# Seven block products in part of down, q, k and v, with q and k computed token-major

## The chip, the cores and the metric

The kernel runs on one core of one Trainium2 chip. The metric is device time in microseconds, the median of several runs; three runs of the kernel before gave 1916.19 us (1915.48 to 1917.2).

## The reference

The reference is a decoder trunk of two layers on 256 tokens of width 2048, in float32. Layer 0 mixes tokens with a causal pooling mixer, layer 1 with differential attention; each is followed by a SwiGLU FFN of width 5632, and the result is normalised.

```python
h = h + pool_mixer(rmsnorm(h), pool_w, pool_scale)              # layer 0
h = h + (silu(n @ wg) * (n @ wu)) @ wd                          # n = rmsnorm(h)
h = h + diff_attention(rmsnorm(h), w_qkv, ..., w_o)             # layer 1
h = h + (silu(n @ wg) * (n @ wu)) @ wd
out = rmsnorm(h, final_norm)
# diff_attention, for each of 8 heads: q and k have two parts of 128, v has 256 columns
p_c = softmax(q_c k_c^T * 128 ** -0.5 - slope * distance, causal)    # c = 0, 1
o = rmsnorm((p_0 - lam * p_1) v, subln_g) * (1 - lambda_init)
```

## The kernel before, in words

**The split.** Every weight and every operand is held as two parts that TensorE multiplies at full rate, a rounded high part and the rest as a low part. A product of two blocks is three matmuls: high x high, high x low, low x high. A weight tile `raw` of 128 x 2048 (1 MB) comes by DMA; `halves` (L105 to L110) rounds it on ACT (`whi`, L108) and subtracts on DVE (`wlo`, L109). Both have three buffers, and so has `raw`.

**Groups.** A group (L128 to L164) makes a result of 256 tokens x 1024 columns: four blocks C11, C12, C21, C22 of 128 tokens x 512 columns in four PSUM banks. It runs over steps of 256 rows of the weight, eight of them for most matrices. A plain step has eight block products, 24 matmuls of 512 columns. A step in seven products has seven block products (the scheme of Strassen in Winograd's form), 21 matmuls; it needs sums of weight blocks (`tsum`, L114 to L117, split into `thi` on ACT and `tlo` on DVE, L120 and L121) and sums of operand blocks. Its products go to seven banks M1, M6, M7, P5, P3, P4, M2, of which the last three are shared with the plain steps as C12, C21 and C11; the eighth bank, X, takes C22 of the plain steps. A group with such steps uses all eight PSUM banks, and `combined` (L166 to L193) makes the four blocks from them, with two copies on ACT and eight adds on DVE. `SEVEN` names the steps: 0, 1 and 4, in gate/up only.

**PSUM.** There are eight banks. `acc` turns through banks 0 to 4, `aux` through 5 to 7. In a group C11, C12, C21 and C22 stand in banks 6, 4, 5 and 7, and M1, M6, M7, P5 in 0 to 3. Transposes, scores and small products take banks from `aux`.

**Stages.** The pooling mixer (L252 to L329) fills `x_tok`, the residual, and transposes it into the operand of FFN 0. An FFN (L331 to L392) has 11 gate/up groups of eight steps, in chunks of 4, 4 and 3. After each the gate goes through Silu on ACT, is multiplied by up on DVE (L351), transposed by TensorE (L357) and split (L359, L360). After a chunk two down groups of 8, 8 or 6 steps are added to `x_tok` (L374). The last chunk also squares `x_tok` and transposes it into the next operand. In attention, q and k were computed unit by unit with the weight as the stationary operand (`product`, L419 and L421): 32 units of 1 MB, each 16 matmuls of 512 columns and 16 of 256, so that q and k come out already transposed, in banks 0 to 4. The two halves of a unit's result are added (L471 to L477) and k is scaled by a row. After a head's four units come its scores (L487), softmax (L489 to L503) and the transposes of its probabilities (L437). Then two groups of v, in plain steps, each followed by four heads (L519 to L535), and two groups of the output product.

**Order.** The program is written stage after stage, and a scheduler puts each engine's instructions into one fixed queue, by readiness in its own model and by priority; a buffer that is still in use holds back the instruction that wants it. The engines run these queues strictly in order, with semaphores between them. So an instruction that waits holds back all that stands behind it on its engine.

Of the kernel before, what the change touches and what calls it, by code (L numbers as in the profile page):

```python
# [16 lines left out]
P = 128  # L17
# [6 lines left out]
H = 8  # L24
# [10 lines left out]
SEVEN = (0, 1, 4)  # L35
# [9 lines left out]
def trunk_kernel(ctx, tc, x_t, x_n, gains, scale_in, final_in, subln, lam_in, band, dist,  # L45
# [41 lines left out]

    def operand(seven=()):

        return [resid.tile([P, 2, 8, P] if p in seven else [P, 2, 2, S], F32R, name="xp", tag=f"xp{p}")  # L90
                for p in range(NP)]
# [20 lines left out]
    def sums(pool, raw):  # L112
        t = pool.tile([P, 4, 512], F32, name="tsum")
        nc.vector.tensor_tensor(t[:, T1:T3 + 1], raw[:, B11:B22 + 1],  # L114
                                raw[:, B12:B12 + 1].broadcast_to([P, 2, 512]), ALU.add)
        nc.vector.tensor_tensor(t[:, T2], t[:, T1], raw[:, B22], ALU.add)
        nc.vector.tensor_tensor(t[:, T4], t[:, T2], raw[:, B21], ALU.add)  # L117
        hi = pool.tile([P, 4, 512], F32R, name="thi")
        lo = pool.tile([P, 4, 512], F32R, name="tlo")
        nc.scalar.copy(hi, t)  # L120
        nc.vector.tensor_tensor(lo, t, f32(hi), ALU.subtract)  # L121
        return hi, lo
# [5 lines left out]
    def group(steps, seven_pool=None):  # L128
# [37 lines left out]
    def combined(ps, pool=None):  # L166
# [3 lines left out]
        get = lambda name, tag, bufs: pool.tile([P, 512], F32, name=name, tag=tag, bufs=bufs)  # L170
        m1 = get("m1", "m", 2)
        nc.scalar.copy(m1, ps[M1])
        u2 = get("u2", "u", 2)
        nc.vector.tensor_tensor(u2, ps[M6], m1, ALU.add)
        c11 = get("c11", "c", 4)
        nc.vector.tensor_tensor(c11, ps[M2], m1, ALU.add)
        u3 = get("u3", "u", 2)
        nc.vector.tensor_tensor(u3, ps[M7], u2, ALU.add)
        p5 = get("p5", "m", 2)
        nc.scalar.copy(p5, ps[P5])  # L180
        q = get("q", "q", 2)
        nc.vector.tensor_tensor(q, p5, u2, ALU.subtract)
        c12 = get("c12", "c", 4)
        nc.vector.tensor_tensor(c12, ps[P3], q, ALU.add)
        c21 = get("c21", "c", 4)
        nc.vector.tensor_tensor(c21, ps[P4], u3, ALU.add)
        q2 = get("q2", "q", 2)
        nc.vector.tensor_tensor(q2, p5, u3, ALU.subtract)
        if X not in ps:
            return [[c11, c12], [c21, q2]]  # L190
        c22 = get("c22", "c", 4)
        nc.vector.tensor_tensor(c22, ps[X], q2, ALU.add)
        return [[c11, c12], [c21, c22]]  # L193
# [31 lines left out]

    def transposed(xp, j, gain, seven=()):

        for p in (2 * j, 2 * j + 1):
            ps = aux((P, 2, 2, P))
            for i in range(2):  # L230
                cols = slice((2 * p + i) * P, (2 * p + i + 1) * P)
                for t in range(2):
                    at = 1 - t if p in seven else t
                    nc.tensor.transpose(ps[:, i, at], x_tok[:, t, cols], ident)
            g = [gain_sb[:, gain, 2 * p + i:2 * p + i + 1] for i in range(2)]
            if p not in seven:
                for i in range(2):
                    split(xp[p][:, i], ps[:, i].rearrange("p t s -> p (t s)"), g[i])
                continue
            e = tmp.tile([P, 8, P], F32, name="e", bufs=1)  # L240

            nc.scalar.activation(e[:, A21:A11 + 1], ps[:, 0], AF.Copy, scale=g[0])
            nc.scalar.activation(e[:, A22], ps[:, 1, 0], AF.Copy, scale=g[1])
            nc.scalar.activation(e[:, A12], ps[:, 1, 1], AF.Copy, scale=g[1])
            nc.vector.tensor_tensor(e[:, S1:S3 + 1], e[:, A21:A11 + 1], e[:, A22:A21 + 1], ALU.subtract)
            nc.vector.tensor_tensor(e[:, S2], e[:, S1], e[:, A11], ALU.subtract)
            nc.vector.tensor_tensor(e[:, S4], e[:, A12], e[:, S2], ALU.add)
            nc.scalar.copy(xp[p][:, 0], e)
            nc.vector.tensor_tensor(xp[p][:, 1], e, f32(xp[p][:, 0]), ALU.subtract)
# [81 lines left out]
    def ffn(layer, xq, ss, seven, next_op, next_gain):  # L331
# [3 lines left out]
        with tc.tile_pool(name=f"ffn{layer}", bufs=1, reuse_waits="tile") as hp:  # L335
            g0 = 0
            for c, n in enumerate(CHUNKS):
                last = c == len(CHUNKS) - 1
                hp_tiles = []
                if last and next_op is None:  # L340
                    final_sb = [hp.tile([P, 1024], F32, name="final_sb", tag=f"h3_{i}") for i in range(2)]
                    for i in range(2):
                        nc.scalar.dma_start(out=final_sb[i], in_=final_in[:, i * 1024:(i + 1) * 1024])
                for g in range(g0, g0 + n):
                    ps = group([(xq[p], p in seven, w_gu[layer][g, p]) for p in range(NP)], hp)
                    cs = combined(ps, hp)
                    h = hp.tile([P, 2, 512], F32, name="h")
                    for t in range(2):
                        a = cs[t][0] if seven else hp.tile([P, 512], F32, name="silu", bufs=2)
                        nc.scalar.activation(a, cs[t][0], AF.Silu, scale=r[:, t:t + 1])  # L350
                        nc.vector.scalar_tensor_tensor(h[:, t], cs[t][1], r[:, t:t + 1], a, ALU.mult, ALU.mult)  # L351
                    for i in range(2):
                        ht = hp.tile([P, 2, 2, S], F32R, name=f"h{g - g0}_{i}")
                        tp = aux((P, 2, S))
                        for k in range(2):
                            for t in range(2):
                                nc.tensor.transpose(tp[:, k, t * P:(t + 1) * P],  # L357
                                                    h[:, t, (2 * i + k) * P:(2 * i + k + 1) * P], ident)
                        nc.scalar.copy(ht[:, :, 0], tp)  # L359
                        nc.vector.tensor_tensor(ht[:, :, 1], tp, f32(ht[:, :, 0]), ALU.subtract)  # L360
                        hp_tiles.append(ht)
                for o in range(2):
# [5 lines left out]
                    ps = group([(hp_tiles[i], False, w_down[layer][o, 2 * g0 + i]) for i in range(2 * n)])  # L368
                    cs = combined(ps, hp)
                    for b in range(2):  # L370
# [6 lines left out]
                        if last and next_op is not None:  # L377
                            transposed(next_op, j, next_gain)
                g0 += n
            if next_op is None:  # L380

                r = row_scale(ss_next)
                for j in range(4):
                    cols = slice(j * 512, (j + 1) * 512)
                    y = hp.tile([P, 2, 512], F32, name="y", tag=f"h{j // 2}_{j % 2}")
# [8 lines left out]
    xp = operand()  # L394
    ss = ffn(0, xq, ss, SEVEN, xp, 3)
# [3 lines left out]
    with tc.tile_pool(name="attn", bufs=1, reuse_waits="tile") as ap_, ExitStack() as heads:  # L399
        at = heads.enter_context(tc.tile_pool(name="attn_tmp", bufs=2, reuse_waits="tile"))  # L400
        v_sb = ap_.tile([P, 2, D], F32, name="v_sb")
        r_col = row_scale(ss)
        qk = ap_.tile([P, 4, S], F32, name="qk0", tag="qk", bufs=8)
        qs_col = ap_.tile([P, 2], F32, name="qs_col")
        subln_sb = ap_.tile([P, 2], F32, name="subln_sb")
        nc.sync.dma_start(out=subln_sb, in_=subln)
        lam_sb = ap_.tile([P, 4], F32, name="lam_sb")
        nc.sync.dma_start(out=lam_sb, in_=lam_in)
        nc.vector.tensor_scalar(qs_col, r_col, QK_SCALE, None, ALU.mult)
        r = None  # L410
        neg_lam = None
        aT = []

        def product(src, acts):

            ps = acc((P, 2, S))
            hi, lo = (x.rearrange("p b (u n) -> p (b u) n", n=P) for x in halves(load(src)))
            for k, a in enumerate(acts):
# [221 lines left out]
```

## Time and profile before

| what | value |
|---|---|
| median of three runs | 1916.19 us |
| the profiled execution | 1915.97 us |
| its span | 1914.2 us |
| granted TensorE clock, mean | 0.993 |
| TensorE busy | 1871.7 us, 98% |
| VectorE busy | 1344.9 us, 70% |
| ScalarE busy | 921.3 us, 48% |

PE is TensorE, PEld its weight loads, DVE VectorE, ACT ScalarE, SP the queue that issues the DMAs. The span goes from the first to the last instruction of one profiled execution. A row of the groups by line has the line, the engine, the operation, what is written <- what is read, the shapes and the count, then busy us and mean ns of one, and the idle time ahead with what ended it. A row of the stages has the window, its length, and for PE, PEld, DVE, ACT and POOL busy us and count, then the granted clock (1 is full), the share of the DMA engines and GB/s. A row of the timeline has start, length, engine and line; in brackets stands the idle time before it and who ended it. Matmuls overlap in the records (each lasts some 390 ns there and the next starts after some 228), so the spacing of starts is what a matmul costs.

### The profile page before, as it was taken

The numbers are of one execution on the slowest core, as the hardware profiler recorded it, in microseconds if no ns is written. First come the engines' busy times: TensorE is split into PE (matmuls) and PEld (weight loads), VectorE is DVE, ScalarE is ACT, GpSimd is POOL, SyncE is SP. The second block draws the span as 40 slices with busy tenths as digits, with TensorE's granted clock in tenths as the row PEclk, the third lists the DMA queues.
The fourth block names the chain that finished last, engine by engine and source line by source line (L and its number), as shares of the span: only waits on it lengthen the run. The fifth ranks groups of instructions, "written<-read, shape, count | busy, mean of one in ns | idle before, by whom it ended". The sixth has DMA issues, their size and how long they took to land.

```text
span 1914.2 us, 20836 instructions
## 1 busy us (share of the span) xinstructions
PE 1871.7 (98%) x8508; PEld 1526.5 (80%) x8508; DVE 1344.9 (70%) x1311; ACT 921.3 (48%) x892; POOL 0.7 (0%) x6
## 2 busy tenths in 40 slices
PE   8899999999999999999999999999999999999997
PEld 5678888888888888888887787788888888888886
DVE  5898756888558975666654356898558897468854
ACT  5555534455434545544445545555434554345543
POOL 0000000000000000000000000000000000000000
PEclk9999999999999999999999999999999999999999
DMA  7455555555556564555553454555555556565552
GB/s 284 154 198 198 197 180 198 195 198 198 195 188 211 176 207 169 177 174 177 174 186 137 139 176 157 189 203 199 198 195 201 198 176 211 185 219 198 198 194 92
DMA packets 51151, 358.83 MB, mean 187 GB/s; under 512 B 6000, under 2 KB 6256, under 8 KB 8432
## 3 DMA queue, kind: packets, MB, share of 16 engines
q1 hardware_dynamic: 50080, 355.36, 53.3%
q10 hardware_dynamic: 976, 2.15, 0.3%
q8 instruction: 66, 1.08, 0.2%
q14 instruction: 29, 0.24, 0.0%
HBM read 355.39 MB, written 2.10 MB: 187 GB/s over the span
## 4 chain that ended last, share of the span: by engine, by line
PE 93%; DVE 3%; ACT 2%; DMA 1%; issue 1%; SPq 0%; DVEq 0%; ACTq 0%
PE b L162 80%; PE b L419 6%; PE b L421 3%; PE b L357 1%; DVE wlo L109 1%; ACT whi L108 1%; DMA x_tok<-x_n 1%; PE b L297 1%; PE b L487 1%; ACT sq L212 0%; PE b L533 0%; PE b L307 0%; DVE xp L224 0%; DMA raw<-w_gu 0%; ACT o_sq L525 0%
## 5 line engine op out<-in xcount | busy, mean ns | idle before, releaser
L109 DVE TENSOR_TENSOR wlo<-raw,whi 128x2048 fp32r<-128x2048 f32 (+1 forms) x331 | 721.3, 2182 | 354.8 <-ACT whi L108 354.0
L108 ACT CAST whi<-raw 128x2048 fp32r<-128x2048 f32 (+1 forms) x331 | 603.1, 1825 | 607.6 <-PE b L162 511.1
L162 PE MATMUL b<-whi,xp 128*128 128x512 f32 x2412 | 768.4, 392 | 6.5 <-DVE xp L224 3.9
L162 PEld LDWEIGHTS b<-whi,xp 128*128 128x128 f32 x2412 | 453.2, 188 | 104.4 <-issue 5.1
L162 PE MATMUL b<-wlo,xp 128*128 128x512 f32 x1206 | 470.7, 390 | 1.8 <-DVE wlo L109 1.8
L162 PE MATMUL b<-whi,h 128*128 128x512 f32 x1408 | 438.3, 391 | 0.0
L162 PEld LDWEIGHTS b<-whi,h 128*128 128x128 f32 x1408 | 263.7, 188 | 56.8 <-DVE h L360 2.1
L162 PE MATMUL b<-wlo,h 128*128 128x512 f32 x704 | 274.2, 390 | 0.1
L162 PEld LDWEIGHTS b<-wlo,xp 128*128 128x128 f32 x1206 | 226.9, 188 | 50.0 <-DVE wlo L109 3.0
L121 DVE TENSOR_TENSOR tlo<-tsum,thi 128x2048 fp32r<-128x2048 f32 x66 | 151.1, 2290 | 52.6 <-ACT thi L120 51.7
L162 PE MATMUL b<-thi,xp 128*128 128x512 f32 x528 | 185.1, 397 | 2.4 <-ACT thi L120 2.3
L419 PE MATMUL b<-xp,whi 128*128 128x512 f32 x512 | 183.1, 402 | 0.0
L120 ACT CAST thi<-tsum 128x2048 fp32r<-128x2048 f32 x66 | 126.1, 1910 | 99.5 <-DVE tsum L117 77.0
L162 PEld LDWEIGHTS b<-wlo,h 128*128 128x128 f32 x704 | 132.2, 188 | 27.3 <-DVE wlo L109 0.5
L421 PE MATMUL b<-xp,wlo 128*128 128x256 f32 x512 | 138.0, 280 | 0.0
L162 PEld LDWEIGHTS b<-thi,xp 128*128 128x128 f32 x528 | 97.2, 189 | 28.7 <-ACT thi L120 10.9
L419 PEld LDWEIGHTS b<-xp,whi 128*128 128x128 f32 x512 | 95.0, 188 | 19.8
L162 PE MATMUL b<-tlo,xp 128*128 128x512 f32 x264 | 105.4, 399 | 0.0
L421 PEld LDWEIGHTS b<-xp,wlo 128*128 128x128 f32 x512 | 96.6, 189 | 2.6
L162 PE MATMUL b<-whi,oT 128*128 128x512 f32 x256 | 81.5, 397 | 0.5 <-DVE xp L224 0.5
L114 DVE TENSOR_TENSOR tsum<-raw 128x1024 f32<-128x1024 f32 x66 | 80.5, 1220 | 0.6
L162 PEld LDWEIGHTS b<-tlo,xp 128*128 128x128 f32 x264 | 50.0, 189 | 13.7 <-DVE tlo L121 3.2
(122 smaller groups left out, 1016.7 us busy)
## 6 DMA issues: line engine op xcount, KB each, us to landing
raw<-w_gu SPq DMA_DIRECT2D x176, 1024.0 KB, 4.8
raw<-w_down SPq DMA_DIRECT2D x88, 1024.0 KB, 4.8
raw<-w_qk SPq DMA_DIRECT2D x32, 1024.0 KB, 4.8
raw<-w_v SPq DMA_DIRECT2D x16, 1024.0 KB, 4.8
raw<-w_o SPq DMA_DIRECT2D x16, 1024.0 KB, 4.8
raw<-pool_w SPq DMA_DIRECT2D x3, 1024.0 KB, 16.9
x_tok<-x_n SPq DMA_DIRECT2D x1, 2048.0 KB, 14.2
xf<-x_t SPq DMA_DIRECT2D x3, 512.0 KB, 10.8
```

Of the source, the lines that this page charges most:

```text
L108: nc.scalar.copy(hi[:, lo_block:], raw[:, lo_block:])
L109: nc.vector.tensor_tensor(lo[:, lo_block:], raw[:, lo_block:], f32(hi[:, lo_block:]), ALU.subtract)
L114: nc.vector.tensor_tensor(t[:, T1:T3 + 1], raw[:, B11:B22 + 1], raw[:, B12:B12 + 1].broadcast_to([P, 2, 512]), ALU.add)
L120: nc.scalar.copy(hi, t)
L121: nc.vector.tensor_tensor(lo, t, f32(hi), ALU.subtract)
L162: nc.tensor.matmul(ps[b], x, y[:, block], start=first, stop=(left[b] == 0))
L297: nc.tensor.matmul(zp[g][t], u, w[:, k % 4], start=(k % 4 == 0 and i == 0), stop=(k % 4 == 3 and i == 2))
L357: nc.tensor.transpose(tp[:, k, t * P:(t + 1) * P], h[:, t, (2 * i + k) * P:(2 * i + k + 1) * P], ident)
L419: big = lambda: nc.tensor.matmul(ps.rearrange("p a s -> p (a s)"), hi[:, k], a.rearrange("p a s -> p (a s)"), start=(k == 0), stop=(k == N ...
L421: small = lambda: nc.tensor.matmul(ps[:, 0, :], lo[:, k], a[:, 0, :], start=False, stop=False)
L487: nc.tensor.matmul(sc[:, :nk], qk[:, c, qb * P:(qb + 1) * P], qk[:, 2 + c, :nk], start=True, stop=True)
```

## The change

**Where the seven products are.** In gate/up the seven steps are now 1, 4 and 6. In each down group they are steps 1 and 4, in each group of q and k and of v steps 1 and 4; the output product stays plain. The transposes that make the operands go through one helper, `pair`, for `x_tok`, the product of gate and up and the attention output alike; for a seven step it forms the sums of operand blocks (`e`) on ACT and DVE.

**q and k.** The units are gone. There are four groups of q and k like the others, with 512 columns of q as the left blocks and 512 of k as the right ones, so one group holds two heads. Its blocks are combined (in place, in four tiles of one buffer each), scaled by row on ACT, transposed by TensorE (L470) and copied by ACT (L472); then each head runs as before, with the scale already in q. The heads are written behind their group, ahead of the next.

**Smaller edits.** `combined` works in place. The sums of a seven step are made ahead of the split of the same tile. The scalars of attention share one tile. The gate and up product is written over up. The probabilities have three blocks in place of four, v stays in the combined tiles.

```diff
-SEVEN = (0, 1, 4)
+SEVEN = (1, 4, 6)
+SEVEN_DOWN = (1, 4)
+SEVEN_QKV = (1, 4)
+SEVEN_O = ()
...
             raw = load(src)
+            t = sums(pool, raw) if seven else None
             w = [halves(raw, B11 if seven else 0)]
             if seven:
-                w.append(sums(seven_pool, raw))
+                w.append(sum_halves(pool, t))
...
+        m1, u2, u3, p5 = (pool.tile([P, 512], F32, name=f"c{i}") for i in ("11", "12", "21", "22"))
         nc.scalar.copy(m1, ps[M1])
         nc.vector.tensor_tensor(u2, ps[M6], m1, ALU.add)
+        nc.vector.tensor_tensor(m1, ps[M2], m1, ALU.add)
         nc.vector.tensor_tensor(u3, ps[M7], u2, ALU.add)
         nc.scalar.copy(p5, ps[P5])
+        nc.vector.tensor_tensor(u2, p5, u2, ALU.subtract)
+        nc.vector.tensor_tensor(p5, p5, u3, ALU.subtract)
+        nc.vector.tensor_tensor(u2, ps[P3], u2, ALU.add)
+        nc.vector.tensor_tensor(u3, ps[P4], u3, ALU.add)
+        if X in ps:
+            nc.vector.tensor_tensor(p5, ps[X], p5, ALU.add)
+        return [[m1, u2], [u3, p5]]
...
+    def pair(dst, src, gains, seven):
+        ps = aux((P, 2, 2, P))
+        for i in range(2):
+            for t in range(2):
+                nc.tensor.transpose(ps[:, i, 1 - t if seven else t], src(i, t), ident)
...
+        e = tmp.tile([P, 8, P], F32, name="e", bufs=1)
+        for i, at in ((0, slice(A21, A11 + 1)), (1, slice(A22, A12 + 1, A12 - A22))):
+            nc.scalar.activation(e[:, at], ps[:, i], AF.Copy, scale=1.0 if gains is None else gains[i])
+        nc.vector.tensor_tensor(e[:, S1:S3 + 1], e[:, A21:A11 + 1], e[:, A22:A21 + 1], ALU.subtract)
+        nc.vector.tensor_tensor(e[:, S2], e[:, S1], e[:, A11], ALU.subtract)
+        nc.vector.tensor_tensor(e[:, S4], e[:, A12], e[:, S2], ALU.add)
+        nc.scalar.copy(dst[:, 0], e)
+        nc.vector.tensor_tensor(dst[:, 1], e, f32(dst[:, 0]), ALU.subtract)
...
-                    ps = group([(hp_tiles[i], False, w_down[layer][o, 2 * g0 + i]) for i in range(2 * n)])
-                    cs = combined(ps, hp)
+                    cs = combined(group([(hp_tiles[i], i in SEVEN_DOWN, w_down[layer][o, 2 * g0 + i])
+                                         for i in range(2 * n)], hp), hp)
...
-                big = lambda: nc.tensor.matmul(ps.rearrange("p a s -> p (a s)"), hi[:, k], a.rearrange("p a s -> p (a s)"),
-                                               start=(k == 0), stop=(k == NK - 1))
-                small = lambda: nc.tensor.matmul(ps[:, 0, :], lo[:, k], a[:, 0, :], start=False, stop=False)
...
-            for i in range(4):
-                ps = product(w_qk[h * 4 + i], acts)
-                if i == 1 and probs is not None:
-                    transpose_probs(h - 1, probs)
...
+        for g in range(4):
+            cs = combined(group([(xp[p], p in SEVEN_QKV, w_qk[g, p]) for p in range(NP)], ap_), ap_)
+            for t in range(2):
+                for b, scale in enumerate((qs_col, r_col)):
+                    nc.scalar.activation(cs[t][b], cs[t][b], AF.Copy, scale=scale[:, t:t + 1])
+            for u in range(2):
+                qk = at.tile([P, 2, 2, S], F32, name="qk", bufs=3)
+                for b in range(2):
+                    tp = aux((P, 2, S))
+                    for c in range(2):
+                        for t in range(2):
+                            nc.tensor.transpose(tp[:, c, t * P:(t + 1) * P],
+                                                cs[t][b][:, (2 * u + c) * P:(2 * u + c + 1) * P], ident)
+                    nc.scalar.copy(qk[:, b], tp)
+                head(2 * g + u, qk)
...
-            cs = combined(group([(xp[p], False, w_v[g, p]) for p in range(NP)]))
+            cs = combined(group([(xp[p], p in SEVEN_QKV, w_v[g, p]) for p in range(NP)], ap_), ap_)
```

More of the change, by code (lines that the diff above doesn't have):

```diff
@@ L224, in split @@
         nc.vector.scalar_tensor_tensor(dst[:, 1, :], src, gain, f32(dst[:, 0, :]), ALU.mult, ALU.subtract)
+    def pair(dst, src, gains, seven):
[3 more added lines that the diff above has]
+                nc.tensor.transpose(ps[:, i, 1 - t if seven else t], src(i, t), ident)
+        if not seven:
+            if gains is None:
+                both = ps.rearrange("p i t s -> p i (t s)")
+                nc.scalar.copy(dst[:, :, 0], both)
+                nc.vector.tensor_tensor(dst[:, :, 1], both, f32(dst[:, :, 0]), ALU.subtract)
+            else:
+                for i in range(2):
+                    split(dst[:, i], ps[:, i].rearrange("p t s -> p (t s)"), gains[i])
+            return
+        e = tmp.tile([P, 8, P], F32, name="e", bufs=1)
[6 more added lines that the diff above has]
+        nc.vector.tensor_tensor(dst[:, 1], e, f32(dst[:, 0]), ALU.subtract)
@@ L226, in transposed @@
     def transposed(xp, j, gain, seven=()):
         for p in (2 * j, 2 * j + 1):
[L229 to L239, printed above, removed]
@@ L248, in transposed @@
-            nc.scalar.copy(xp[p][:, 0], e)
-            nc.vector.tensor_tensor(xp[p][:, 1], e, f32(xp[p][:, 0]), ALU.subtract)
+            pair(xp[p], lambda i, t: x_tok[:, t, (2 * p + i) * P:(2 * p + i + 1) * P],
+                 [gain_sb[:, gain, 2 * p + i:2 * p + i + 1] for i in range(2)], p in seven)
     xp = operand()
```

181 lines of the change are left out of this document (52 added, 129 removed).

## The prediction

> **What bounds the kernel now.** I read the page first, then the table of stages (the windows), then the chain of waits, then the groups by line and shape, and last the timeline of the places that the change touches.
>
> The page gives the span, PE's busy time and the chain that ended last.
>
> ```profile
> span 1914.2 us, 20836 instructions
> PE 1871.7 (98%) x8508; PEld 1526.5 (80%) x8508; DVE 1344.9 (70%) x1311; ACT 921.3 (48%) x892; POOL 0.7 (0%) x6
> PE 93%; DVE 3%; ACT 2%; DMA 1%; issue 1%; SPq 0%; DVEq 0%; ACTq 0%
> ```
>
> PE is the bound: 93% of the chain is matmul time. A matmul that goes away takes its whole slot with it, unless PE then waits for something else. In the stages (start:end, length, PE, weight load, DVE, ACT, POOL, granted clock, DMA) PE is full in a gate/up group and in the stretch of q and k, and only the seams have holes.
>
> ```profile
> 628.00:671.00 43.00, 43.00 (x197) 35.25 (x196) 38.30 (x34) 22.98 (x18) 0.00 (x0) 1.00 0.57 196
> 782.00:975.00 193.00, 193.00 (x1116) 168.54 (x1115) 126.75 (x232) 91.24 (x151) 0.00 (x0) 1.00 0.50 173
> 1180.00:1206.00 26.00, 22.24 (x99) 16.36 (x98) 21.18 (x30) 17.56 (x24) 0.00 (x0) 0.99 0.47 161
> ```
>
> DVE, the second engine, stands at 38.3 of 43 us in a gate/up group, so seven-product steps already run it near full. The slot of a matmul comes from the chain of waits (start, length): 548 matmuls in 124.70 us are **0.2276 us** each. Below it are the scores of two heads that lie seven heads apart: (974.12 - 805.50) / 7 = **24.09 us a head**.
>
> ```profile
> 242.36 124.70 PE b L162 x548
> 805.50 0.66 PE b L487 x4
> 974.12 0.66 PE b L487 x4
> ```
>
> **The change part by part.** The profiled execution took 1915.97 us with a span of 1914.2, and the median of the runs is 1916.19, 0.2 above it; the sum is made against 1915.97.
>
> *Down and v.* A seven-product step has 21 matmuls for 24. Down has 12 groups with two such steps each, 72 matmuls less, -16.4 us; v has two groups, 12 less, -2.7 us. What they add lies on DVE and ACT: sums of weights, their split, and the recombination.
>
> ```profile
> L109 DVE TENSOR_TENSOR wlo<-raw,whi 128x2048 fp32r<-128x2048 f32 x265 | 606.5, 2289 | 349.1 <-ACT whi L108 349.0
> L109 DVE TENSOR_TENSOR wlo<-raw,whi 128x1536 fp32r<-128x1536 f32 x66 | 115.7, 1753 | 5.7 <-ACT whi L108 5.0
> L121 DVE TENSOR_TENSOR tlo<-tsum,thi 128x2048 fp32r<-128x2048 f32 x66 | 151.1, 2290 | 52.6 <-ACT thi L120 51.7
> L114 DVE TENSOR_TENSOR tsum<-raw 128x1024 f32<-128x1024 f32 x66 | 80.5, 1220 | 0.6
> L117 DVE TENSOR_TENSOR tsum<-tsum,raw 128x512 f32<-128x512 f32 x66 | 45.5, 690 | 1.6
> ```
>
> A plain step costs DVE 2.29 us against 5.46 of PE (24 slots); a seven step costs 1.75 + 2.29 + 1.22 + 2 x 0.69 = 6.64 against 4.78. A down group of eight steps is then 2 x 6.64 + 6 x 2.29 + 8 recombining adds and 4 adds to x_tok at 0.69 = 35.3 us of DVE for 42.3 of PE. It fits, and since the M banks are complete after step 4, five adds run under the last steps. The six-step group of the last chunk is 30.7 for 31.4: it fits without slack.
>
> *q and k, the work of PE.* Before, two heads take 48.2 us. After, a group of two heads has 186 matmuls (42.3 us), 16 transposes of q and k, 6 of the probabilities, and 8 scores. Timeline rows: six transposes from 241.49 to 242.11 are 0.10 each; four scores are 0.47 + 0.55 (each pair starts here and the next L419 at 805.80 and 807.65).
>
> ```profile
> 241.49 0.87 PE L357 MATMUL b<-ident,h 128*128 128x128 f32 x6
> 242.11 0.48 PE L162 MATMUL b<-whi,h 128*128 128x512 f32 x1
> 805.33 0.82 PE L487 MATMUL b<-qk 128*128 128x128 f32 x4
> 805.80 0.58 PE L419 MATMUL b<-xp,whi 128*128 128x512 f32 x1
> 807.10 0.89 PE L487 MATMUL b<-qk 128*128 128x128 f32 x4
> 807.65 0.58 PE L419 MATMUL b<-xp,whi 128*128 128x512 f32 x1
> ```
>
> 42.3 + 2.2 + 2.0 = 46.6 us for 48.2, so -1.6 x 4 = -6.1 us (unrounded) if nothing waits. The DVE of a group: before, 126.75 / 193 x 48.2 = 31.7. Three kinds of x16 like the row below go (12 of 0.42 a group), two seven steps (+8.7) and eight adds (+5.5) come: 40.8 of 46.6.
>
> ```profile
> L476 DVE TENSOR_TENSOR k_s<-b,q_c 128x256 f32<-128x256 f32 x16 | 6.7, 420 | 14.5 <-ACT q_c L471 14.5
> ```
>
> The loads cost nothing either way: 32 of 1 MB before and after, in the same queue.
>
> ```profile
> raw<-w_qk SPq DMA_DIRECT2D x32, 1024.0 KB, 4.8
> ```
>
> *q and k, the waits.* Here the order changes most. Before, products of q and k used banks 0 to 4, and heads 5 to 7. On PE, two scores stand among unit products that need nothing of the head:
>
> ```order
> L419 MATMUL b2_5444<-xp_449,whi_5447 128x512
> L421 MATMUL b2_5444<-xp_449,wlo_5448 128x256 x2
> L419 MATMUL b2_5444<-xp_449,whi_5447 128x512
> L487 MATMUL b7_5490<-qk0_5294 128x128 [waits DVE_49,PE_49]
> L487 MATMUL b6_5517<-qk0_5294 128x256 [waits Activation_49]
> L419 MATMUL b3_5545<-xp_442,whi_5548 128x512 [waits Activation_49]
> ```
>
> After, on PE at the second head of the first group (a_sb are the probabilities, qk the transposed q and k, xp_439 the next group's first step):
>
> ```order
> L470 MATMUL b5_5794<-ident_75,c22_5696 128x128
> L423 MATMUL b6_5781<-ident_75,a_sb_5751 128x128 [waits DVE_49]
> L438 MATMUL b7_5813<-qk_5787 128x128 [waits Activation_49]
> L438 MATMUL b5_5829<-qk_5787 128x256 [waits PE_49]
> L423 MATMUL b6_5781<-ident_75,a_sb_5778 128x128 [waits DVE_49]
> L423 MATMUL b6_5781<-ident_75,a_sb_5778 128x128
> L438 MATMUL b6_5802<-qk_5787 128x128 [waits PE_49,Activation_49]
> L438 MATMUL b6_5840<-qk_5787 128x256 [waits DVE_49]
> L172 MATMUL b5_5883<-whi_5865,xp_439 128x512 [waits DVE_49]
> L172 MATMUL b5_5883<-wlo_5866,xp_439 128x512
> L172 MATMUL b5_5883<-whi_5865,xp_439 128x512
> L172 MATMUL b6_5869<-whi_5865,xp_439 128x512 [waits DVE_49]
> ```
>
> A group now takes all eight banks, so the next group's banks 5, 6, 7 are closed until the heads give them back. Nothing stands between these head rows, and five of the eight wait for DVE or ACT. Their cost from rows (DVE neighbours overlap by some 0.08 us: 857.04 + 0.48 is past 857.43):
>
> ```profile
> 857.04 0.48 DVE L489 SCALAR_TENSOR_TENSOR s_sb<-b,qs_col,bias 128x256 f32<-128x256 f32 x1
> 857.43 0.15 DVE L496 RECIPROCAL l_inv<-l_sum 128x1 f32<-128x1 f32 x1
> L491 DVE TENSOR_REDUCE m_neg<-s_sb 128x1 f32<-128x256 f32 x16 | 6.5, 404 | 0.0
> L494 ACT ACTIVATE p_sb<-s_sb,m_neg 128x256 f32<-128x256 f32 x16 | 8.0, 503 | 20.1 <-DVE m_neg L491 20.1
> L503 DVE SCALAR_TENSOR_TENSOR a_sb<-p_sb,l_inv 128x256 f32<-128x256 f32 x8 | 3.9, 485 | 0.3
> L438 ACT COPY aT<-b 128x256 f32<-128x256 f32 x8 | 3.0, 375 | 1.9 <-PE b L437 1.9
> ```
>
> I walked the three queues by hand from the group's last matmul (0). The sums c11, c12, c21 are done before 0, because DVE waits there only for ACT's casts; c22 at 2.4; then one wlo (2.2) and the first tsum (1.2) keep DVE until 5.8, when it takes the first scores. PE has 27 matmuls, 16 transposes and four scores until 9.2, with holes of 0.3 in all. Then it waits 0.4 for a_sb (9.5), 0.9 for ACT's copy of q and k, which queues behind two exps (10.5), 0.4 for the next a_sb (11.4), 0.8 until ACT has taken bank 6, 0.5 and 0.8 for the scores to be read (13.1, 14.2). At 17.7 both heads are done, with 13.6 us of PE work in it: **4.1 us idle a group, +16.5 us** for four (the last before v's first group). DVE then owes the next weight split, done at 22.7; PE has matmuls until 24.1. Bounds: 2 us, if handovers are quicker than I took them, and 9, if each costs more and the holes add up. The nearest row is the heads after v's first half, where a chain over the same engines leaves PE 4.2 of 16 us idle, so I keep 4.1.
>
> ```profile
> 1021.00:1037.00 16.00, 11.79 (x54) 8.58 (x53) 7.71 (x27) 12.07 (x37) 0.00 (x0) 1.00 0.30 110
> ```
>
> Such holes can cost clock too. After v's second half PE waits 1.43 and 0.93 us in short succession, and then the granted clock is 0.57 for four us:
>
> ```profile
> 1090.37 0.91 PE L533 MATMUL b<-ident,o_n 128*128 128x128 f32 x4 [1.43 <-ACT o_n L529]
> 1092.21 1.04 PE L533 MATMUL b<-ident,o_n 128*128 128x128 f32 x4 [0.93 <-ACT o_n L529]
> 1092.50:1096.50 4.00, 3.96 (x13) 3.20 (x13) 1.45 (x3) 1.34 (x4) 0.00 (x0) 0.57 0.00 0
> ```
>
> 0.43 x 4 us is 1.7 us lost each time. In v's first half (row above) the clock stayed at 1.00, so I take 0.6 x 4 x 1.7 = **+4**. The Trainium skill ("TensorE: Matmul & The Clock Gate", Part 1 and the table "Why this matters for your kernels") states that the clock drops after an idle window of about 3.4 us and warns of gaps over some 3 us; by that rule the heads, with no hole over 1 us, lose nothing. The row above disagrees: holes of 1.43 and 0.93 were enough. What the rule would make of the time is a rival below.
>
> *Gate/up.* The steps in seven products are 1, 4, 6 for 0, 1, 4: equal work, other order. Before, at the seam, a new group opened bank 0, which is free early (names as above):
>
> ```order
> L162 MATMUL b7_873<-whi_1007,xp_98 128x512
> L162 MATMUL b0_1090<-whi_1078,xp_91 128x512 [waits Activation_49]
> L162 MATMUL b0_1090<-wlo_1079,xp_91 128x512 [waits DVE_49]
> L162 MATMUL b0_1090<-whi_1078,xp_91 128x512
> L162 MATMUL b6_1094<-whi_1078,xp_91 128x512 [waits DVE_49]
> ```
>
> After, PE opens banks 6 and 4 at once and then wants c12, the product of gate and up:
>
> ```order
> L172 MATMUL b7_795<-whi_1003,xp_98 128x512
> L172 MATMUL b6_1071<-whi_1067,xp_91 128x512 [waits DVE_49,Activation_49]
> L172 MATMUL b6_1071<-wlo_1068,xp_91 128x512
> L172 MATMUL b6_1071<-whi_1067,xp_91 128x512 x2
> L172 MATMUL b4_1078<-whi_1067,xp_91 128x512 [waits DVE_49]
> L231 MATMUL b7_1050<-ident_75,c12_1032 128x128 [waits DVE_49]
> ```
>
> The reader sees 11 matmuls (2.5 us) ahead of the transpose. By the same walk DVE ends the last tlo at -10.3, bank 6's add at -3.3, bank 4's at 0.9, c12 at 2.1: **0**, with 0.4 us to spare. If DVE is 0.8 us later, 22 groups cost +9.
>
> *Seams.* At o to FFN 1 and at the start of FFN 0 the first step is now plain, and its PE work covers the sums of step 1.
>
> ```profile
> 1187.69 0.47 PE L162 MATMUL b<-whi,xp 128*128 128x512 f32 x1 [1.01 <-DVE xp L224]
> 1194.02 1.20 PE L162 MATMUL b<-thi,xp 128*128 128x512 f32 x4 [0.93 <-ACT thi L120]
> 1203.62 1.20 PE L162 MATMUL b<-thi,xp 128*128 128x512 f32 x4 [1.12 <-ACT thi L120]
> 1205.43 1.60 PE L162 MATMUL b<-whi,xp 128*128 128x512 f32 x3 [0.61 <-ACT whi L108]
> 1206.00:1208.00 2.00, 2.00 (x6) 1.62 (x5) 2.00 (x1) 0.00 (x0) 0.00 (x0) 0.50 0.03 8
> 62.00:64.00 2.00, 0.65 (x5) 0.41 (x4) 2.00 (x5) 1.70 (x6) 0.00 (x0) 1.00 0.00 0
> 66.00:68.00 2.00, 2.00 (x6) 1.52 (x6) 1.74 (x7) 0.91 (x2) 0.00 (x0) 0.50 0.00 0
> ```
>
> These holes are 3.7 us and a clock loss of 1.7; about 1.5 stays (bank 5 waits for the splits of x_tok), -3.9. The start has some 2.9 and 1.7 of the same kind; I take -3.1. Together **-7** (bounds -10 and 0). At FFN 0 to q/k the other way: x_tok and two e chains come later by the adds, step 1's tsum waits behind them, **+3.5** with the last chunk (0 to +8). At the end one add more stands before the last x_tok add: **+0.6**.
>
> Sum: -16.4 - 2.7 - 6.1 + 16.5 + 4 + 0 - 7 + 3.5 + 0.6 = -7.6, so 1908.4, with the 0.2 to the median 1908.6.
>
> **The rivals.**
> *Heads exposed (slower).* The walk's waits each come longer, since a group's heads sit on one chain over three engines and PE's queue is in order. For it: five waits in eight rows. Against it: of other work only two short sums of weights stand inside the heads on DVE, none on ACT. It decides from 4.1 + (7.6 + 3.8) / 4 = 7 us idle a group; at 9 us and with a clock loss each time it is 1908.6 + 19.6 + 2.8 = 1931. Chance 0.22.
> *DVE becomes the bound in down.* The last chunk's groups have 30.7 for 31.4 us, and in FFN 0 the splits of x_tok come on top: three plain pairs of two like the row below, and a seven pair of about 2.2 us (estimated from the rows of its shapes above), 5.1 of DVE for 1.6 of PE, 2.8 too much in each of two groups. That gives 1914. Against: the adds under the last step already use DVE's idle time. Chance 0.16.
>
> ```profile
> L224 DVE SCALAR_TENSOR_TENSOR xp<-b,gain_sb,xp 128x256 fp32r<-128x256 f32 x36 | 15.8, 477 | 1.6 <-ACT xp L223 1.6
> ```
>
> *The waits are hidden.* PE's matmuls cover the heads but for 1 us a group, clock kept: 1908.6 - 12.4 - 4 = 1892. Chance 0.10.
> *No clock loss.* The heads keep the full clock as in v's first half: 1904.6. Chance 0.12; this is where the skill's rule would put it.
>
> **How the numbers follow.** The forecast itself has 0.40; its own range is 1902 to 1915. About 0.2% (3.8 us) is what a measurement of this kernel can tell from no change. Faster than 1912.4: most of the forecast (0.34), both hidden cases (0.22) and a little of DVE's (0.04): 0.60. Within: the rest of the forecast and DVE's case, 0.18. Slower: 0.22. The range, 1891 to 1930, holds the hidden heads at its lower end and the exposed ones nearly at its upper.
>
> **What would show it.** Right: PE matmuls of down, v and q/k fewer by 84 and replaced as counted; two heads in some 51 us, with PE idle of 3 to 6 us after each group of q and k, released by DVE a_sb and s_sb and ACT's copies; gate/up groups still at some 43 us; the holes at 62 to 68 and 1187 to 1208 smaller. Wrong: gate/up groups over 43.3 us, down groups of eight steps over 43, idle per group of heads under 2 or over 7, or a granted clock of one half in other places.

## The result and the profile after

The kernel after took 1900.91 us (median of four runs, 1899.33 to 1903.71) against 1916.63 for the kernel before: ratio 0.9921, 95% interval 0.9909 to 0.9933, or -15.1 us (0.8%) where -7.6 was forecast. The profiled execution took 1902.04. The page now reads:

```profile
span 1900.1 us, 20741 instructions
PE 1852.9 (98%) x8204; PEld 1506.3 (79%) x8204; DVE 1571.1 (83%) x1591; ACT 1013.6 (53%) x983; POOL 0.7 (0%) x6
PE 92%; DVE 4%; ACT 2%; issue 1%; DMA 1%; SPq 0%; DVEq 0%; ACTq 0%
```

PE is still the bound. DVE has 226 us more to do. In the chain of waits (start, length) the transposes behind two gate/up groups of FFN 0, and the long stretch of matmuls in the second, third and fourth group of q and k and in the first group of v:

```profile
366.36 0.66 PE b L231 x6
409.09 0.66 PE b L231 x6
...
834.69 33.15 PE b L172 x145
885.55 33.17 PE b L172 x145
936.42 33.11 PE b L172 x145
988.27 33.11 PE b L172 x145
```

A gate/up group takes 42.7 us. From one of these stretches to the next, a group with its two heads, it is 50.9, 50.9 and 51.9 us, where the forecast had some 51. The timeline of PE at the second head of the second group:

```profile
877.72 0.92 PE L438 MATMUL b<-qk 128*128 128x128 f32 x4 [0.43 <-ACT qk L472]
878.78 0.44 PE L423 MATMUL b<-ident,a_sb 128*128 128x128 f32 x2
879.85 0.49 PE L438 MATMUL b<-qk 128*128 128x128 f32 x2 [0.63 <-ACT aT L425]
880.73 0.70 PE L438 MATMUL b<-qk 128*128 128x256 f32 x2 [0.38 <-DVE s_sb L440]
881.64 0.50 PE L172 MATMUL b<-whi,xp 128*128 128x512 f32 x1 [0.21 <-DVE s_sb L440]
```

PE stands in this order, in front of ACT's copies and the scores being read, as walked. The brackets sum to 1.65 us, yet 878.78 to 879.85 is 1.07 us for two transposes: a record ends later than the slot it needs, so part of a wait lies under it. The granted clock (next to last but two) behind three such stretches:

```profile
828.00:832.00 4.00, 3.59 (x9) 2.60 (x10) 3.21 (x15) 1.81 (x8) 0.00 (x0) 0.59 0.00 0
880.00:884.00 4.00, 3.40 (x15) 2.38 (x16) 3.39 (x17) 1.97 (x8) 0.00 (x0) 1.00 0.02 4
982.00:986.00 4.00, 3.62 (x10) 2.60 (x10) 3.43 (x16) 1.97 (x8) 0.00 (x0) 0.57 0.00 0
```

It drops in the first and last group, not in the two between (from 930 to 934 us it is 1.00 too). At the seam from o to FFN 1, PE's waits from 1180 to 1290 in the kernel before (total, times, longest):

```profile
PE b L162 <- ACT thi L120: 2.0, 2, 1.1
PE b L162 <- DVE xp L224: 1.0, 1, 1.0
PE b L162 <- DVE wlo L109: 0.9, 1, 0.9
PE b L162 <- ACT whi L108: 0.6, 1, 0.6
```

and all that is left at the same place in the kernel after:

```profile
PE b L172 <- DVE xp L224: 0.5, 1, 0.5
```

### The profile page after: what moved, and what is told of

It is laid out like the page before. It is cut to its first block, busy times and chain, and to the rows that moved or that the text cites. A ratio compares the mean times of both kernels' runs of the same rounds, so it can differ in the third digit from the quotient of the medians.

```text
span 1900.1 us, 20741 instructions
## 1 busy us (share of the span) xinstructions
PE 1852.9 (98%) x8204; PEld 1506.3 (79%) x8204; DVE 1571.1 (83%) x1591; ACT 1013.6 (53%) x983; POOL 0.7 (0%) x6
## 4 chain that ended last, share of the span: by engine, by line
PE 92%; DVE 4%; ACT 2%; issue 1%; DMA 1%; SPq 0%; DVEq 0%; ACTq 0%
PE b L172 88%; PE b L231 2%; DVE wlo L115 1%; DMA x_tok<-x_n 1%; PE b L303 1%; ACT sq L212 1%; ACT whi L114 1%; PE b L313 0%; PE b L438 0%; DVE tsum L120 0%; DVE y L386 0%; DVE x_tok L373 0%; DVE s_sb L440 0%; DVE oT L224 0%; DVE xp L224 0%
## 5 line engine op out<-in xcount | busy, mean ns | idle before, releaser
L172 PE MATMUL b<-whi,xp 128*128 128x512 f32 x2804 | 905.8, 393 | 8.8 <-DVE c L189 3.0
L172 PEld LDWEIGHTS b<-whi,xp 128*128 128x128 f32 x2804 | 526.9, 189 | 126.9 <-ACT e L244 5.7
L172 PE MATMUL b<-wlo,xp 128*128 128x512 f32 x1402 | 549.9, 392 | 0.6 <-DVE wlo L115 0.5
L172 PE MATMUL b<-whi,h 128*128 128x512 f32 x1168 | 370.3, 390 | 1.1 <-ACT e L244 1.1
L130 DVE TENSOR_TENSOR tlo<-tsum,thi 128x2048 fp32r<-128x2048 f32 x102 | 233.1, 2286 | 19.8 <-ACT thi L129 19.3
L172 PE MATMUL b<-wlo,h 128*128 128x512 f32 x584 | 227.5, 390 | 0.1
L129 ACT CAST thi<-tsum 128x2048 fp32r<-128x2048 f32 x102 | 194.8, 1910 | 30.7 <-DVE tsum L123 30.7
L122 DVE TENSOR_TENSOR tsum<-tsum,raw 128x512 f32<-128x512 f32 x102 | 70.4, 690 | 2.4
L123 DVE TENSOR_TENSOR tsum<-tsum,raw 128x512 f32<-128x512 f32 x102 | 70.1, 687 | 1.9
L172 PEld LDWEIGHTS b<-tlo,xp 128*128 128x128 f32 x312 | 58.6, 188 | 12.1 <-DVE tlo L130 0.2
L172 PE MATMUL b<-thi,h 128*128 128x512 f32 x192 | 67.6, 393 | 0.3 <-ACT thi L129 0.3
L172 PEld LDWEIGHTS b<-whi,oT 128*128 128x128 f32 x256 | 49.2, 193 | 12.9 <-issue 2.6
```

Source lines behind the costliest of these rows:

```text
L172: nc.tensor.matmul(ps[b], x, y[:, block], start=first, stop=(left[b] == 0))
```

## The experiments

The runs were made in sets, each beside runs of the kernel before (medians 1915.0 to 1917.3). So kernels are compared by their ratios to it, times 1917; a difference of two kernels is uncertain by some 3 us (by 4 where `units` is one of them).

### The order of the steps

**order_014.**

```diff
-SEVEN = (1, 4, 6)
+SEVEN = (0, 1, 4)
```

> The kernel after, with the seven-product steps of gate/up put back to 0, 1 and 4. Theory A (the order of the steps is what the forecast missed: with steps 0 and 1 side by side PE stands 0.1 to 0.2 us at a time in front of tlo, thi and wlo, some 0.25 us a group, which the records hide because a matmul's record is longer than its slot): gate/up and its seams lose about 5.7 us, the start 1.7, o to FFN 1 4.6, together +12, about 1913 where the kernel after has 1901, and the slot of a matmul in the first two steps of a gate/up group is over 0.23 us again. Theory B (the gain in gate/up comes from the shorter recombination in place and the shared helper, not from the order): at most the +7 that the forecast gave the two seams, 1901 to 1908, and gate/up groups stay as they are now.

1916.29 us, ratio 0.9999 (0.9991 to 1.0008). With the old order the whole change is worth nothing: all 15.0 us (0.0078) hang on three numbers. That is theory A, and more than its 12. Where they lie is read from the chain: the transposes after the second and the last gate/up group of both FFNs with steps 0, 1, 4

```profile
155.56 0.66 PE b L231 x6
707.54 0.66 PE b L231 x6
1287.07 0.66 PE b L231 x6
1839.80 0.66 PE b L231 x6
```

and with steps 1, 4, 6, in the kernel after:

```profile
154.52 0.66 PE b L231 x6
706.07 0.66 PE b L231 x6
1277.05 0.66 PE b L231 x6
1828.66 0.66 PE b L231 x6
```

With the old order the first and third mark stand one matmul (0.23 us) earlier in PE's queue, the others fifteen (3.4 us). So the new order gains 1.3 us at the start, 0.4 + 3.2 = 3.6 within FFN 0, 8.6 - 3.2 = 5.4 between the FFNs, 1.1 + 3.2 = 4.3 within FFN 1, and loses 0.3 at the end: 14.3, the difference of the two spans. Within the FFNs PE's list of waits shows next to nothing for the 7.9 us: for `order_014` no wait from 160 to 705 us and 0.2 us from 1285 to 1825, for the kernel after none.

**before_146.** The same edit the other way, on the kernel before.

```diff
-SEVEN = (0, 1, 4)
+SEVEN = (1, 4, 6)
```

> The kernel before, with the seven-product steps of gate/up moved to 1, 4 and 6 and nothing else. Theory A: the order alone brings about 12 us, 1904.6 where the kernel before has 1916.6. Theory B: only the seams that the forecast named, 7 us at most, 1909.6 or more.

1897.75 us, ratio 0.9901 (0.9888 to 0.9915): 19 us, faster than the kernel after. The same transposes in the kernel before:

```profile
154.88 0.70 PE b L357 x6
715.83 0.88 PE b L357 x6
1279.52 0.70 PE b L357 x6
1840.16 0.87 PE b L357 x6
```

and with steps 1, 4, 6:

```profile
150.72 0.66 PE b L357 x6
707.53 0.68 PE b L357 x6
1265.41 0.66 PE b L357 x6
1822.23 0.67 PE b L357 x6
```

With the new order the transposes stand six matmuls (1.4 us) later in the queue at the first and third mark, one at the others. So the start gives 4.2 + 1.4 = 5.5 us; within FFN 0 560.95 against 556.81 us, 4.1 less the 1.1 by which the marks have moved, 3.0; within FFN 1 in the same way 2.7; between them 6.9, and 0.2 at the end, which makes the 18.4 of the spans. The forecast had 3.1 for the start, 3.9 for o to FFN 1, and none for the groups within. The start is uncertain: the granted clock from 0 to 110 us was 0.95 in the one profile and 0.98 in the other, which alone is 3.3 us. What the old order loses there is in the timeline of the kernel before, at step 1 of the third group and, in FFN 1, at the front of the second:

```profile
161.58 0.39 PE L162 MATMUL b<-whi,xp 128*128 128x512 f32 x1
161.98 1.20 PE L162 MATMUL b<-thi,xp 128*128 128x512 f32 x4
...
1238.22 0.50 PE L162 MATMUL b<-wlo,xp 128*128 128x512 f32 x1 [0.88 <-DVE wlo L109]
```

From 161.58 to the next start are 0.40 us where a slot is 0.23, in front of thi. No idle time is printed, since the record lasts 0.39. In the rest of this group (to 194 us) one more delay of this kind stands, 0.39 us in front of tlo of step 4 at 174.53, and none in steps 5 to 7.

**before_046 and before_126.** Is it the seven-product step at the front, or two side by side?

The kernel before, first with 0, 4, 6 and then with 1, 2, 6:

```diff
-SEVEN = (0, 1, 4)
+SEVEN = (0, 4, 6)
```

```diff
-SEVEN = (0, 1, 4)
+SEVEN = (1, 2, 6)
```

> The kernel before, with the seven-product steps of gate/up at 0, 4 and 6: one of them opens the group, none stands beside another. Moving them to 1, 4 and 6 brought 19 us (1897.8 against 1917.1). Theory N (the loss comes from two such steps side by side, 13.3 us of DVE for 9.6 of PE, so that every thi, tlo and wlo behind them is late): most of the 19 us is there with 0, 4, 6 too, 1898 to 1901. Theory S (the loss comes from opening a group with such a step: at the start, at o to FFN 1 and at the seams between groups its operand sums and weight sums have no PE work in front of them): most of the loss stays, 1909 to 1916.

> The kernel before, with the seven-product steps of gate/up at 1, 2 and 6: two side by side, but behind a plain step of 24 matmuls. Theory N: most of the loss stays, 1909 to 1917. Theory S: most of the 19 us is there, 1898 to 1903.

1898.14 us (0.9901) and 1902.43 us (0.9927, 0.9915 to 0.9939). By the totals theory N holds for the first and fails for the second, theory S the reverse: neither alone makes the 19 us. A seven-product step that opens the group alone costs nothing in sum, two side by side behind a plain step cost some 5 us. The stages say more. The transposes after the second and the last gate/up group of FFN 0 with steps 0, 4, 6 and then with 1, 2, 6:

```profile
147.05 0.66 PE b L357 x6
705.32 0.67 PE b L357 x6
...
150.41 0.65 PE b L357 x6
710.55 0.68 PE b L357 x6
```

That is 558.27 and 560.14 us against 556.81 with 1, 4, 6; the second holds three more matmuls (0.7 us). So within FFN 0 the order 0, 4, 6 loses 1.5 us and 1, 2, 6 loses 2.6, where 0, 1, 4 loses 3.0 (FFN 1 in the same way: 1.4, 3.0 and 2.7). Inside the FFNs the steps side by side cost about what the old order costs. The greater part of the 19 us, 5.5 + 6.9 = 12.4 at the start and between the FFNs, comes only with two of them opening the group, since the totals of the other two orders leave no loss for these places. The product in front of FFN 1 is plain and in front of FFN 0 stands no group, so a recombination that DVE still owes cannot be the main reason there; the waits listed at that seam are for xp, thi, whi and wlo. Why one at the front alone costs nothing there is not shown. All three quick orders also end on step 6 and the slow one on step 4; an order such as 0, 1, 6, which would part the two, was not run. The delays found in the third group, at steps 1 and 4 and not behind them, speak against it but do not settle it.

### Parts of the change undone

**down_plain.**

```diff
-SEVEN_DOWN = (1, 4)
+SEVEN_DOWN = ()
```

> The kernel after, with all steps of down plain (72 matmuls more). Theory A (down in seven products is worth its matmuls, as the forecast has it): 72 x 0.2267 = +16.3 us, 1917 where the kernel after has 1901. Theory B (it gives part of that back: the operand sums and the recombination stand in DVE's way at the last chunk, where q and k wait for them, and at the end): the kernel with the old units and the new order of steps differs from the kernel before with that order by -9.3 only, so +9 to +10, 1910 to 1911.

1911.62 us, ratio 0.9984 (0.9975 to 0.9992): down in seven products is worth 12.1 us, between the theories. The forecast's own terms for it, -16.4 + 3.5 + 0.6, give -12.3. Its +3.5 is the seam from FFN 0 to q and k. From 700 to 860 us, the heads left out, PE's listed waits are 0.2 us in the kernel before, 2.9 in the kernel after (1.1 for ACT's e, 1.0 for xp, 0.5 for wlo, 0.3 for thi), and 1.2 with down plain. So only about half of the seam goes with down, and that 12.1 meets 12.3 so closely is in part luck.

**units.** The kernel after with the old code of q, k and v:

```diff
-        for g in range(4):
-            cs = combined(group([(xp[p], p in SEVEN_QKV, w_qk[g, p]) for p in range(NP)], ap_), ap_)
...
+        for h in range(H):
+            for i in range(4):
+                ps = product(w_qk[h * 4 + i], acts)
...
```

> The kernel after, with q and k computed unit by unit as before and v in plain steps; down, gate/up and all else as after. Theory A (q and k token-major cost 12.8 us net over the four groups, and the seam from FFN 0 to them 3.6, since PE waits in its order for the heads' chain although the records show only 1.7 us idle a group; v's seven steps bring 2.7): 1901 - 12.8 - 3.6 + 2.7 = 1887. Theory B (the chain of the heads is mostly covered, as the recorded idle time says: PE's work -6.1, idle +7, clock +2, so +3 net): 1901 - 3 - 3.6 + 2.7 = 1897.

1888.45 us, ratio 0.9863 (0.9843 to 0.9882): -11.1 us by ratio, -12.5 by the medians. Theory A, though by little more than the noise. Token-major q and k cost about what the forecast said, 14.4 less v's 2.7 = 11.7, and most of it does not stand in the brackets of the timeline. The seam's listed waits do not go with it: 2.7 us are left of the 2.9.

**qkv_plain.** Plain blocks must leave PSUM before they can be transposed, so they go through tiles of their own.

```diff
-SEVEN_QKV = (1, 4)
+SEVEN_QKV = ()
...
-                    nc.scalar.activation(cs[t][b], cs[t][b], AF.Copy, scale=scale[:, t:t + 1])
+                    nc.scalar.activation(cs[t][b], ps[t][b], AF.Copy, scale=scale[:, t:t + 1])
```

> The kernel after, with all steps of q, k and v plain, and q and k still token-major (36 matmuls more; the four blocks of a group go from their banks through ACT into tiles of their own). Theory A (the seven steps of q, k and v are worth their matmuls): 36 x 0.2267 = +8.2 us, 1909. Theory B (they are given back: without them DVE has 14 us less to do in a group of two heads, the operand of the first group needs no sums, and the heads' chain is shorter): 1899 to 1903.

1918.96 us, ratio 1.0017 (1.0008 to 1.0026): +18.4 us, far above both theories. The stages of the heads in groups 1 to 4, and of v's first heads:

```profile
822.00:842.00 20.00, 17.38 (x68) 12.82 (x68) 10.37 (x40) 7.95 (x24) 0.00 (x0) 0.83 0.15 52
874.00:894.00 20.00, 17.20 (x80) 12.57 (x81) 11.10 (x39) 9.97 (x26) 0.00 (x0) 1.00 0.26 99
927.00:947.00 20.00, 17.85 (x75) 12.79 (x74) 11.18 (x39) 9.37 (x26) 0.00 (x0) 0.83 0.27 102
980.00:1000.00 20.00, 17.18 (x84) 12.38 (x82) 12.15 (x38) 10.37 (x28) 0.00 (x0) 1.00 0.29 105
1038.00:1058.00 20.00, 14.76 (x55) 10.69 (x54) 7.80 (x28) 12.49 (x37) 0.00 (x0) 0.81 0.20 75
```

PE idles 15.6 us in these five rows, and three of them lose 3.4 to 3.8 us of clock, 10.6 in all. The kernel after has such losses too: in its stretches of the same stages (20 us each from 820, 871, 922, 973 and 1023) PE idles 11.6 us and the clock is 0.91, 1.00, 1.00, 0.91 and 0.93, which is 5.0 us. So 4.0 us of idle time and 5.6 of clock are added, and with the 8.2 of the matmuls that makes 17.8 of the 18.4. This is an account from one profile each, not a proof; why plain steps make the heads wait longer is open.

### The heads' waits

**heads_low_46.** Transposes of q and k, scores and probabilities turn through banks 0 to 3.

```diff
+    def low(shape=(P, 512)):
+        turn["aux"] += 1
+        return bank(turn["aux"] % 4, shape)
...
-                    sc = aux()
+                    sc = low()
...
-SEVEN_QKV = (1, 4)
+SEVEN_QKV = (4, 6)
```

> The kernel after, with the transposes of q and k, the scores and the transposes of the probabilities in banks 0 to 3 in place of 5 to 7, and the seven-product steps of q, k and v at 4 and 6. The next group can then open its banks 4 to 7 for four plain steps (96 matmuls, 21.8 us) while the heads run. Theory A (the cost of the heads is that nothing may stand between them because all banks are taken): some 4.3 us a group come back and the clock is kept, 4 x 4.3 + 2 = 19 us, 1882 to 1886. Theory B (the chain over DVE and ACT is the limit, and the next group's weights wait behind it on these engines whichever bank they use): PE only waits elsewhere, 1897 to 1903.

1893.86 us, ratio 0.9882 (0.9867 to 0.9898): -7.5, between the theories. The groups take 47.8 us and the clock over q and k (780 to 1010 us) stays at 1.00, as theory A has it. Some of the gain is lost beside them. At v's heads (1010 to 1110) the clock is 0.91 where the kernel after has 0.95, 4 us. And from the last transposes of FFN 0's gate/up (705.42 us) to the first scores (820.95) are 115.5 us where the kernel after has 114.6 (705.91 to 820.47): with steps 4 and 6 the seam from FFN 0 is 1 us longer, not the 4.3 us that the next expectation gives for it.

**heads_low_14.** The same, with `SEVEN_QKV = (1, 4)`.

> As the run with the heads in banks 0 to 3, but the seven-product steps of q, k and v stay at 1 and 4, so that the next group has one plain step (24 matmuls, 5.4 us) to cover the heads before it wants banks 0 to 3. With steps 4 and 6 a group of two heads took 47.8 us instead of 50.9, but the seam from FFN 0 to q and k became 4.3 us longer. Theory A (one plain step covers most of the waits, which sum to some 3 us; the longer seam came from the steps 4 and 6): groups of 48 to 48.5 us, the seam as in the kernel after, 1889 to 1891. Theory B (the waits only move to step 1, which finds banks 0 to 3 taken): groups of 50 us or more, 1897 to 1902.

1886.53 us, ratio 0.9854 (0.984 to 0.9867): -12.8, more than theory A had. The first scores come at 819.10 us. From 780 to 1010 us no wait of PE is left. The first scores of each group, in the chain (which begins a little behind the instruction's start):

```profile
819.26 1.33 PE b L442 x8
866.85 1.33 PE b L442 x8
914.68 1.33 PE b L442 x8
962.54 1.33 PE b L442 x8
```

A group takes 47.8 us. So the waits that went were 50.9 - 47.8 = 3.0 us a group, and PE's own work is 47.8 at most. One plain step of 24 matmuls covers them.

**all_low.** The heads of v in banks 0 to 3 too.

```diff
-                op = aux((P, 2, E))
+                op = low((P, 2, E))
...
-    def pair(dst, src, gains, seven):
-        ps = aux((P, 2, 2, P))
+    def pair(dst, src, gains, seven, turn_of=aux):
+        ps = turn_of((P, 2, 2, P))
```

> As the run with the heads in banks 0 to 3 and steps 1 and 4, and the eight heads of v in banks 0 to 3 as well, so that the next group of v, or of the output product, can open banks 4 to 7 while they run. In the kernel after PE waits 4.5 us for oT, 3.7 for o_n and 1.3 in front of their first product, 9.5 in all, and the clock drops behind the second half (some 1.7 us). Theory A (banks again): the output product has four plain steps that need only the first half's heads, v's second group one plain step: 6 to 9 us less than 1886.5, 1878 to 1880. Theory B (the chain over ACT and DVE from one head to the next, with one buffer for o_n, is the limit, and PE runs out of other work): 1884 to 1887.

1870.71 us, ratio 0.9761 (0.9748 to 0.9775): -17.8 against the run before, twice what theory A had. The waits of PE from 1010 to 1100 us in the kernel after, which are the same in the run before:

```profile
PE b L172 <- DVE oT L224: 4.5, 2, 2.2
PE b L231 <- ACT o_n L497: 3.7, 5, 1.0
PE b L487 <- DVE oT L224: 1.3, 4, 0.4
```

and from 1000 to 1100 in this run:

```profile
PE b L235 <- ACT o_n L501: 0.2, 1, 0.2
```

The 9.5 us of recorded waits are gone. The clock from 1018 to 1036 and from 1074 to 1092 us was 0.81 and 0.91 in the run before and is 1.00 here, which is 5.0 us more. The rest, some 3 us, was not measured by itself.

**units_d146 and all_low_d146.** A third seven-product step in the long down groups.

```diff
-SEVEN_DOWN = (1, 4)
+SEVEN_DOWN = (1, 4, 6)
```

> The kernel with the units of before for q and k, and a third seven-product step in the down groups of eight steps (steps 1, 4 and 6; 24 matmuls less). Theory A (PE bounds down): -24 x 0.2267 = -5.4 us against the same kernel with two steps (1888.5), 1883. Theory B (DVE, by then at 39.7 us of 41.5 in such a group by the forecast's figures, is the bound there, or the group's end waits for it): 1887 to 1890.

> The same with a third seven-product step in the down groups of eight steps (24 matmuls less). With the units of before this gave -4.2 us where the matmuls alone are 5.4. Expected: the run without it less 4 to 5.5 us; if the heads of v come out as theory A has them 1873 to 1876, if as theory B 1879 to 1883.

1884.47 us (0.9841, -4.2) and **1866.07 us** (0.9734, 0.9721 to 0.9747; -5.2): nearer to theory A in the first, and lower than expected in the second only because all_low was. Each difference is hardly above the uncertainty, but both are near the 5.4 us of the matmuls, so DVE does not bound down with three such steps. This last kernel is the fastest of all, 2.7% below the kernel before.

## Why the prediction was right, and where not

**Everything but the order: right, in part by luck.** Without its seam term of -7 the forecast's sum is -0.6; order_014 measures -0.2 (-1.7 to +1.5). Down was -12.3 in the terms and 12.1 in the run; q, k and v +11.7 and 11.1. But with the new order on both sides (before_146 and the kernel after) the rest of the change costs 3.8 us, with some 3 us of uncertainty, so its parts may not simply add up, and the seam from FFN 0, which is in both down's and q and k's cost, is not cleanly parted.

**The order: the mis-sized term.** The forecast took -7 for the two seams (bounds -10 and 0) and wrote **0** for gate/up. Measured by order_014 in the kernel after: 1.3 + 5.4 = 6.7 us at the start and between the FFNs, as forecast, and **7.9** within the FFNs, where the forecast had nothing. (In the kernel before the same edit brings 12.4 and 5.7.) The step that failed is "equal work, other order": I walked the queues only to see whether the new order would lose anything, and took it that the old one lost nothing, because its waits did not show in PE's list of waits. They lay under the matmuls' records (0.40 us from start to start for 0.23). The spacing would have told, as at 161.58.

**The walk of the heads: right in place, a little high.** Forecast 4.1 us idle on 46.6 of work; measured 3.0 on at most 47.8. The waits named (ACT's copy of q and k, the bank behind aT, the scores to be read) are those of the timeline; the extra work lies mostly in the return from transposes or scores to the 512-column matmuls (883.84 to 884.16 in the timeline after is 0.32 us for a slot of 0.23): in heads_low_14, from 866.85 to 914.68, eleven such returns take 0.31 to 0.42 us each. The idle of 3 to 6 us that was to be seen is there in the spacing, but its brackets show only 1.65, below the 2 that was named as wrong. A check on a wait should be put on spacing.

**The clock: half, where it was forecast.** Forecast four losses of 1.7; two were seen, the last group taking 51.9 us where its neighbours take 50.9. More was lost at v's heads, which the forecast left as they were: from 1020 to 1110 us the clock is 0.94 in the kernel after and 0.98 in the kernel before, 3.6 us. One profile each does not show that the change did this: before_146, whose attention is the old one, has 0.96 over the same stage. The Trainium skill ("TensorE: Matmul & The Clock Gate", Part 1) has the clock fall after an idle window of about 3.4 us; no printed hole here is over 0.7 us, and it fell to 0.57, so the rows disagree. The section "A second HAM failure mode: psum-queue depth-cycling" of the same page of the Trainium skill tells of a kernel in which frequent micro-idles between matmul groups make the clock oscillate; the rows agree with that. Part 1 of that page of the Trainium skill calls the activity window free-running, and such a window would let one group lose clock and the next not. That it is the window's phase was not tested.

**Start:** forecast -3.1. The marks give 5.5 for the order in the kernel before but only 1.3 in the kernel after; the granted clock from 0 to 110 us was 0.95 before, 0.98 in before_146, 0.94 in the kernel after and 0.95 in order_014, so much of the difference is the execution's clock, and one profile each can't size it.

**The rivals.** Heads exposed (9 us a group) is excluded by 3.0; DVE as the bound in down's last chunk would have left 12.3 - 5.6 = 6.7 us to lose in down_plain, which lost 12.1; waits hidden by heads_low_14, which finds them. That the heads keep the full clock fell with the rows at 828 and 982.

## What to carry to other kernels

Price the order that is there as carefully as the new one: where two heavy steps side by side open a group, small stalls can lie under the records of the bounding engine, so compare its spacing, stage by stage, with the bare slot. Where heads or other small work stand between large groups, give them banks that the next group wants last; here that brought 12.8 and 17.8 us, where the products saved in down brought 12.1, and it agrees with the Trainium skill ("Perfetto Trace Analysis", Matmuls), which has independent matmul groups rotate through different PSUM banks so that the evacuation of one overlaps the next. A change that bundles several edits should be taken apart: here one line of it was worth the whole, and the rest came to nothing in sum.

## What the runs showed of the hardware

Behind holes of 0.2 to 0.7 us in short succession the granted clock was 0.59 and 0.57 over 4 us (a loss of 1.7 us) in the first and last group of q and k and 1.00 in the two between them (rows at 828, 880 and 982). In the profiles of order_014 (0.58 from 834 to 838 us, 0.63 from 936 to 940) and down_plain (0.61 from 832 to 836, 0.66 from 934 to 938), and in the run with plain q and k, the first and third were hit: which groups lose clock changes from one kernel's profile to the next although their heads are written alike. In the long stretch through a chunk's down groups a matmul of 512 columns takes less than in the row of the forecast (0.2276):

```profile
240.26 123.14 PE b L172 x543
```

That is 0.2268 us, so the forecast's slot held small waits too; where only plain steps stand, the starts in the kernel before lie 0.2267 apart as well.
